# The first expert pair's tokens gathered as rows and then transposed, and the end of the routing in another order

## The chip, the cores and the metric

The kernel runs on one core of a Trainium2 chip. Its time is in device microseconds (us), the median of several runs. The engines are named as in the profile: PE (TensorE), DVE (VectorE), ACT (ScalarE), POOL (GpSimd) and SP (SyncE, which issues most DMAs).

## The reference

One decoder layer over 512 tokens of 1024 features, in float32: two mixers (dilated attention and a spatial gating unit), an output projection, a layer norm (LN1), a mixture of experts and a second layer norm. Here only the seam between LN1 and the experts matters:

```python
h = layer_norm(ALPHA * h + mix, ln1_g, ln1_b)          # 512 x 1024
g_logits = t @ w_group + b_group                        # 4 groups, the best one is taken
e_logits = einsum('td,gde->tge', t, w_expert) + b_expert
top_vals, top_idx = top_k(e_sel, 2)                     # 2 of the 8 experts of that group
gu  = einsum('td,edf->tef', t, w_gate_up[g])            # 1024 -> 2 x 256
act = silu(gu[..., :256]) * gu[..., 256:] * gate
y  += einsum('tef,efd->td', act, w_down[g])             # 256 -> 1024
h = layer_norm(ALPHA * h + y, ln2_g, ln2_b)
```

There are 32 experts. Each token goes to two of them, and all experts' weights are read: 96 MB.

## The kernel before

**Stages.** The input projection, attention and the gating unit come first. Then the output projection works in four tiles of 128 tokens (`i` = 0 to 3, `L` = 3); the first half of the features of all tiles comes first, and the loop at line 954 makes the second half tile by tile and carries LN1 and the routing of the tile before along with it. Behind the loop stands the end of the routing (lines 995 to 1046), then the expert loop over 16 pairs of experts.

**Slots and lists.** Each expert has 64 places, so a pair of experts is one tile of 128 rows. `route_pick` takes a tile's two experts per token (`A`, `Ab`), `route_rank` counts with small matmuls how many tokens went to each expert before (`rks`), `route_slots` makes each token's place, and `pair_sel(p, a, b)` (line 873) writes the 0/1 mask of pair `p` for tiles `a` to `b`, 8 x 128 columns for all four. `pair_list` (line 878) multiplies the mask with `vals` in 8 small matmuls and gives the token numbers (columns 0 to 3) or the gates (3 to 7) of the 128 rows. `pair_tok` turns them into indices, and `gather(p)` fetches the rows from `h_dram` into `xgs[p % 2]` with an indirect DMA that POOL issues.

**The first pair** has no gather. `slots_of(i)` makes `S0[i]` (line 916), the mask of pair 0 for tile `i` (128 tokens x 128 places), and `spread` multiplies with it on PE: `x_sb` of the tile, every eighth column from column `k`, is the stationary operand and `S0[i]` the moving one, so the product is the transposed input of feature block `k`, ready for the gate products. Eight blocks by four tiles make 32 such products. Tiles 0 to 2 are summed in `parts[0]` and `parts[1]`, which ACT copies to `x0f`; tile 3 goes to `parts[2]` and `parts[3]`, and DVE adds it (line 1041).

**The end of tile 3** is a chain over several engines: residual and statistics (DVE, lines 700 and 701), transposes (PE, line 708) with an ACT copy (709), `ln1_stats`, scaling by ACT (734) and POOL (737, 738) for columns 256 to 1023, `logit_mm` (715), `logit_out` (753, 754), `route_pick`, `ln1_rest` for columns 0 to 255 (744, 746), `h_out` (the tile's rows to `h_dram`, by SP), `route_rank`, `route_slots` (843 to 845), `slots_of`.

**The weights** lie in a ring of 21 slots of 1 MB, six fills to a pair. `wfill(n)` issues the fills up to number `n` on SP's queue, each waiting until its slot is free. Slot 19 is the room of `ln1_g` and `ln1_b`; fills 20 and 21 reuse the slots of pair 0's first four gate products (line 905, `k` = 0 to 3); fill 22 needs the room of the routing's tiles, which is closed behind `k` = 7, and the fills after it the slots that pair 0's later products free.

**Order.** From the middle of the output projection the instructions of PE, DVE, ACT, POOL and SP each run in the order in which the program writes them; nothing is rescheduled.

Of the kernel before, what the change touches and what calls it, by code (L numbers as in the profile page):

```python
# [10 lines left out]
F32 = mybir.dt.float32  # L11
# [14 lines left out]
NT = 4  # L26
KD = 8
# [31 lines left out]
def layer(tc, I, out):  # L59
# [41 lines left out]
    def ps_t():  # L101
        return ps_tp.tile([128, 4, 128], F32, name="tp", bufs=2)
# [600 lines left out]
    def r_transpose(i, n):  # L703
        rTs[i, n] = op.tile([128, 4, 128], F32, name="rT", bufs=2)
        tp = ps_t()
        for j in range(4):
            k = n * 4 + j
            pe.transpose(out=tp[:, j], in_=x_sb[:, i, k * 128:(k + 1) * 128], identity=ident)
        act.copy(rTs[i, n], tp)
# [6 lines left out]

    mv1s = {}

    def ln1_stats(i):
        mv1 = op.tile([128, 6], F32, name="mv1", bufs=4)  # L720
        mv1s[i] = mv1
        dve.bn_aggr(mv1[:, 0:2], st1[:, i])
        act.activation(mv1[:, 2:3], mv1[:, 1:2], AF.Sqrt, bias=eps)
        dve.tensor_scalar(mv1[:, 4:5], mv1[:, 0:1], -1.0, None, op0=ALU.mult)
        dve.reciprocal(mv1[:, 3:4], mv1[:, 2:3])
        dve.tensor_tensor(mv1[:, 5:6], mv1[:, 4:5], mv1[:, 3:4], op=ALU.mult)

    def ln1_apply(i, cut):

# [18 lines left out]
    def h_out(i):  # L748
        sp.dma_start(out=h_dram[i * 128:(i + 1) * 128, :], in_=x_sb[:, i])
# [92 lines left out]
    def route_slots(i):  # L842
        dve.tensor_tensor(t2, A[:, i], bc(rks[0][:, i, None, :], [128, 2, NE]), op=ALU.mult)
        dve.tensor_reduce(slot[:, i], t2, axis=AX.X, op=ALU.add)
        dve.tensor_tensor(slotp[:, :, i], bc(slot[:, i, None, :], [128, NPAIR, 2]), bc(iota_p[:, :, None], [128, NPAIR, 2]),
                          op=ALU.add)
# [64 lines left out]
    def slots_of(i):  # L911
        pair_sel(0, i, i + 1)
        if not S0:
            t = op.tile([128, NT, 128], F32, name="S0")
            S0.extend(t[:, j] for j in range(NT))
        dve.tensor_tensor(S0[i], sels[0][:, 2 * i], sels[0][:, 2 * i + 1], op=ALU.add)

    def spread(acc, k, tiles, start=True, stop=True):
        for i in tiles:
            pe.matmul(acc[:, k % 4 * 128:k % 4 * 128 + 128], x_sb[:, i].rearrange("s (q k) -> s k q", k=KD)[:, k], S0[i],  # L920
                      start=(start and i == tiles[0]), stop=(stop and i == tiles[-1]))

    for kk, k in enumerate(KORD):
        if kk == 4:
# [29 lines left out]
    for i in range(NT):  # L954
        for kk in range(KD):
            if i == L - 1 and kk == 4:

                for z in range(2):
                    op_second(L, z)
                wfill(15)  # L960
            op_second(i, kk)
            if i == 1 and kk == 0:
                router_sums()
            if i > 0 and kk == (1 if i < L else 2):
                r_transpose(i - 1, 1)
            if i > 0 and kk == (3 if i < L else 4):
                logit_mm(i - 1, 1)
                logit_out(i - 1)
                route_pick(i - 1, i)
                ln1_apply(i - 1, 512 if i < L else 0)  # L970
                if i < L:
                    ln1_rest(i - 1, 512)
            if i == L and kk == 3:
                wfill(17)
            if i == L and kk == 6:
                wfill(18)
            if kk == 5:
                r_transpose(i, 0)
            if kk == 7:
                logit_mm(i, 0)  # L980
                if i > 0:
                    route_rank(i - 1, i)
        resid(i, 1, acc1[i])
        if i < L:
            ln1_stats(i)
        if i > 0:
            route_slots(i - 1)
            slots_of(i - 1)
            if i < L:
                h_out(i - 1)  # L990
                for p in (1, 2):
                    pair_sel(p, i - 1, i)
        if i < L:
            wfill((13, 14, 16)[i])
    xg12 = opA.tile([128, 2, D], F32, name="xg12", tag="wo3")
    xgs = [xg12[:, p] for p in range(2)]
    h_out(L - 1)
    wfill(19)
    r_transpose(L, 1)
    ln1_stats(L)  # L1000
    xT0 = [op.tile([128, 4, 128], F32, name="rT", bufs=2) for _ in range(2)]
    x0f = [t.rearrange("p k s -> p (k s)") for t in xT0]
    parts = [ps_acc() for _ in range(4)]

    def part(ks):
        for k in ks:
            spread(parts[k // 4], k, range(L))

    ln1_apply(L, 256)
    act.preload_act_table(AF.Exp)  # L1010
    for k in (0, 4):
        spread(parts[k // 4], k, [0, 1], stop=False)
    logit_mm(L, 1)
    logit_out(L)
    route_pick(L, NT)
    for k in (0, 4):
        spread(parts[k // 4], k, [2], start=False)
    part([1, 2, 3])
    act.copy(x0f[0], parts[0])
    ln1_rest(L, 256)  # L1020
    h_out(L)
    route_rank(L, NT)
    route_slots(L)
    slots_of(L)
    part([5, 6, 7])
    act.copy(x0f[1], parts[1])
    for k in range(4):
        spread(parts[2], k, [L])
    for p in (1, 2):
        pair_sel(p, L - 1, NT)  # L1030
    ip0 = ps_t().rearrange("p a b -> p (a b)")
    ips = [ip0[:, 8 * p:8 * p + 7] for p in range(3)]
    for p in (1, 2, 0):
        pair_list(p, ips[p], 0, 3)
    for k in range(4, KD):
        spread(parts[3], k, [L])
    dve.tensor_tensor(emask, rks[0], bc(iota_c[:, None, :], [128, NT, NE]), op=ALU.is_ge)


    for kk in range(2):  # L1040
        dve.tensor_tensor(x0f[kk], x0f[kk], parts[2 + kk], op=ALU.add)
        pair_tok(kk + 1, ips[kk + 1], 1)
        gather(kk + 1)
    pair_tok(0, ips[0], 1)
    route_gates(0, NT)
    act.preload_act_table(AF.Silu)

    gp = ps_acc()
    for k in range(KD):
        gate_up(0, xT0, k, gp)  # L1050
        if k == 3:
            wfill(1 + NSLOT)
        if k == 0:
            pair_sel(3, 0, NT)
        if k == 5:
            cmax_i = route_spill()
        if k == 6:
            for p in range(3):
                pair_list(p, ips[p], 3, 7)
            for p in range(3):  # L1060
                dve.tensor_reduce(tgs[p][:, 1:2], ips[p][:, 3:6], axis=AX.X, op=ALU.add)
                pair_out(p, ips[p])
# [304 lines left out]
```

## Time and profile before

| | |
|---|---|
| median of 3 runs | 501.38 us (501.13 to 502.98) |
| the profiled execution | 501.38 us, its span 499.7 us |
| mean granted PE clock | 0.981 |
| PE busy | 468.3 us (94%) |
| DVE, ACT, POOL busy | 231.0, 162.4, 129.2 us |
| DMA | 141.18 MB, mean 283 GB/s |
| the chain that ended last | PE 65%, DMA 25%, DVE 6% |

Times in the rows count from the span's start. PE is the matmuls, PEld the loads of their stationary operand; a float32 matmul leaves two records of each, and the two halves of a gate product (two experts, 64 places each) run side by side. `PEclk` is the granted clock as a share of 2.4 GHz. A line of the timeline may merge several instructions (x8), and its time then reaches from the first start to the last end.

### The profile page before, as it was taken

How to read it: one execution, taken by the hardware profiler on the slowest of the kernel's cores; microseconds unless marked ns; L12 is line 12 of the kernel's file. 1: busy time of each engine (PE TensorE's matmuls, PEld its weight loads, DVE VectorE, ACT ScalarE, POOL GpSimd, SP SyncE). 2: the span in 40 equal slices, each digit the busy share in tenths (PEclk: the TensorE clock that was granted, in tenths of full speed). 3: DMA queues.
4: the chain of work that ended last, by engine and by line, in shares of the span. 5: the costliest groups of instructions: out<-in, count | busy, mean ns of one | idle time of the engine just before them, and what ended most of it. 6: DMA issues, size and time to landing. Idle time of an engine off the chain costs nothing.

```text
span 499.7 us, 6653 instructions
## 1 busy us (share of the span) xinstructions
PE 468.3 (94%) x2322; PEld 280.8 (56%) x2322; DVE 231.0 (46%) x598; ACT 162.4 (33%) x366; POOL 129.2 (26%) x196
## 2 busy tenths in 40 slices
PE   7999999999899999987999999999998898799994
PEld 5788887888767678867843333333333233243351
DVE  3586637723477638798452222222234331010146
ACT  4543536241478632322112222222221121032243
POOL 4024345000296910344111211111110110000380
PEclk9999999999999999998899999999999999898998
DMA  8844231750298549585589999999999999998464
GB/s 262 288 125 114 63 121 42 221 200 0 65 402 254 190 161 364 201 282 245 169 324 378 428 419 419 419 420 422 421 420 419 420 426 419 419 423 373 151 241 171
DMA packets 40805, 141.18 MB, mean 283 GB/s; under 512 B 10508, under 2 KB 14656, under 8 KB 28993
## 3 DMA queue, kind: packets, MB, share of 16 engines
q1 hardware_dynamic: 35808, 130.71, 68.3%
q0 software_dynamic: 4960, 10.01, 5.5%
q8 instruction: 20, 0.33, 0.3%
q14 instruction: 17, 0.13, 0.1%
HBM read 131.78 MB, written 16.25 MB: 296 GB/s over the span
## 4 chain that ended last, share of the span: by engine, by line
PE 65%; DMA 25%; DVE 6%; ACT 1%; SPq 1%; issue 1%; POOL 1%; ACTq 0%; DVEq 0%
DMA wc<-in_w_gate_up 14%; PE acc L905 13%; DMA wc<-in_w_down 9%; PE acc L320 7%; PE acc L321 7%; PE acc L322 7%; PE acc L1112 6%; PE acc L920 3%; DMA x_sb<-in_x 2%; PE tp L1082 2%; PE acc L605 2%; PE tp L620 2%; PE acc L580 1%; PE acc L582 1%; PE acc L581 1%; PE sc L414 1%
## 5 line engine op out<-in xcount | busy, mean ns | idle before, releaser
L905 PE MATMUL acc<-wc,xTm 128*64 128x512 f32 x464 | 120.6, 608 | 8.3 <-DMA wc<-in_w_gate_up 8.0
L905 PEld LDWEIGHTS acc<-wc,xTm 128*64 128x64 f32 x464 | 33.3, 138 | 72.2 <-issue 52.8
L320 PE MATMUL acc<-w_hi,xTh 128*128 128x512 f32 x160 | 65.1, 407 | 0.8 <-ACT vs_sb L375 0.7
L321 PE MATMUL acc<-w_lo,xTh 128*128 128x512 f32 x160 | 62.9, 393 | 0.4 <-DVE w_lo L312 0.4
L322 PE MATMUL acc<-w_hi,xTl 128*128 128x512 f32 x160 | 62.8, 392 | 0.0
L1112 PE MATMUL acc<-wc,aT 128*64 128x512 f32 x240 | 60.0, 610 | 2.9 <-ACT aT L1097 2.9
L1122 POOL DMA_INDIRECT y_dram<-y,to x15 | 15.8, 1053 | 140.4 <-DVE xTm L1083 74.2
L1120 DVE TENSOR_SCALAR rs<-rs 128x1 f32<-128x1 f32 x15 | 3.2, 214 | 91.9 <-ACT y L1114 91.9
L312 DVE TENSOR_TENSOR w_lo<-w_raw,w_hi 128x512 fp32r<-128x512 f32 x40 | 28.2, 706 | 34.5 <-ACT w_hi L311 34.3
L311 ACT ACTIVATE w_hi<-w_raw 128x512 fp32r<-128x512 f32 x40 | 25.3, 634 | 53.2 <-PE acc L322 47.8
L1112 PEld LDWEIGHTS acc<-wc,aT 128*64 128x64 f32 x240 | 18.6, 140 | 34.3 <-issue 30.3
L1114 ACT ACTIVATE y<-acc 128x512 f32<-128x512 f32 x30 | 17.9, 597 | 60.7 <-PE acc L1112 44.3
L422 POOL TENSOR_TENSOR P<-P,st 128x128 f32<-128x128 f32 (+3 forms) x32 | 23.2, 749 | 50.8 <-DVE st L421 49.3
L320 PEld LDWEIGHTS acc<-w_hi,xTh 128*128 128x128 f32 x160 | 30.2, 189 | 7.8 <-ACT vs_sb L375 1.1
L321 PEld LDWEIGHTS acc<-w_lo,xTh 128*128 128x128 f32 x160 | 30.2, 189 | 6.9 <-DVE w_lo L312 1.4
L1088 DVE SCALAR_TENSOR_TENSOR sa<-sa,tg,acc 128x256 f32<-128x256 f32 x16 | 7.7, 479 | 56.9 <-ACT sa L1087 53.0
L322 PEld LDWEIGHTS acc<-w_hi,xTl 128*128 128x128 f32 x160 | 30.0, 188 | 6.7 <-DVE xTl L163 0.3
L897 POOL DMA_INDIRECT xg<-h_dram,ti x15 | 15.8, 1053 | 56.2 <-DVE ti L894 19.5
L1087 ACT ACTIVATE sa<-acc 128x256 f32<-128x256 f32 x16 | 6.2, 385 | 69.1 <-PE acc L905 69.1
L1082 PEld LDWEIGHTS tp<-ident,xg 128*128 128x128 f32 x120 | 15.1, 194 | 18.7 <-issue 8.9
L873 DVE TENSOR_TENSOR sel<-iota_v,slotp 128x1024 bf16<-128x1024 f32 (+2 forms) x23 | 22.5, 990 | 0.1
L420 ACT ACTIVATE P<-P,st 128x128 f32<-128x128 f32 (+3 forms) x32 | 17.9, 563 | 8.3 <-DVE st L418 8.2
(334 smaller groups left out, 781.0 us busy)
## 6 DMA issues: line engine op xcount, KB each, us to landing
wc<-in_w_gate_up SPq DMA_DIRECT2D x62, 1024.0 KB, 19.2
wc<-in_w_down SPq DMA_DIRECT2D x30, 1024.0 KB, 20.8
w_raw<-in_w_in SPq DMA_DIRECT2D x18, 512.0 KB, 3.7
y_dram<-zeros SPq DMA_DIRECT2D x8, 512.0 KB, 8.0
wo_raw<-in_w_out SPq DMA_DIRECT2D x16, 256.0 KB, 3.5
wc<-y_dram SPq DMA_DIRECT2D x8, 512.0 KB, 9.3
x_sb<-in_x SPq DMA_DIRECT2D x8, 256.0 KB, 9.4
h_dram<-x_sb SPq DMA_DIRECT2D x4, 512.0 KB, 3.0
```

Source lines behind the costliest of these rows:

```text
L311: act.activation(wh, raw, AF.Copy)
L312: dve.tensor_tensor(wl, raw, wh.bitcast(F32), op=ALU.subtract)
L320: pe.matmul(acc[i], xh, wh, start=(k == 0), stop=False)
L321: pe.matmul(acc[i], xh, wl, start=False, stop=False)
L322: pe.matmul(acc[i], xl, wh, start=False, stop=(k == KD - 1))
L420: act.activation(P[:, 0:n], P[:, 0:n], AF.Exp, bias=st4[:, 0:1], scale=-1.0, accum_out=st4[:, 1:2])
L422: pool_e.tensor_tensor(P[:, 0:n], P[:, 0:n], bc(st4[:, 2:3], [128, n]), op=ALU.mult)
L873: dve.tensor_tensor(sels[p][:, 2 * a:2 * b], bc(iota_v.rearrange("p a b -> p (a b)")[:, None, :], [128, n, 128]), bc(slotp[:, p, a:b].rear ...
L905: pe.matmul(gp[zs], xT[k // 4][:, k % 4, zs], w[k % 4 // 2][:, k % 2 * 512:k % 2 * 512 + 512], start=(k == 0), stop=(k == KD - 1))
L1082: pe.transpose(out=tp[:, j], in_=xv[:, kk * 4 + j], identity=ident)
L1112: pe.matmul(dp[n][zs], aT[:, c, zs], w[c][:, ns], start=(c == 0), stop=(c == 1))
L1114: act.activation(y0[:, ns], dp[n], AF.Copy, accum_out=rs[:, n:n + 1])
```

## The change

Tile 0 of pair 0 is still spread. Tiles 1 to 3 are gathered as rows instead: `rows(i, ...)` multiplies the stationary `S0[i]` with 512 columns of `x_sb`, two products to a tile, summed over the three tiles in `parts[2]` and `parts[3]`. ACT and DVE copy the sum into `xgs[0]`, PE transposes it in eight blocks, and DVE adds them to the spread part of tile 0. The masks of pairs 1 and 2 are made for all tiles at once behind the routing, no longer tile by tile in the loop. The ranking and the slots of tile 2 move out of the loop's last turn to behind it, between spreads of tile 0, and the slots stand between the two parts of `ln1_stats(L)`. The list and the gather of pair 1 come ahead of the transposes. The lists of pairs 2 and 0, gather 2, `route_gates` and the table load follow gate product `k` = 1, and pair 3's mask follows `k` = 3. `wfill(20)` stands behind the last `h_out`; fills 20 and 21 stay behind `k` = 3. `ip0` is taken from the pool `ps_s` instead of `ps_t`.

```diff
-    def ln1_stats(i):
-        mv1 = op.tile([128, 6], F32, name="mv1", bufs=4)
-        mv1s[i] = mv1
-        dve.bn_aggr(mv1[:, 0:2], st1[:, i])
-        act.activation(mv1[:, 2:3], mv1[:, 1:2], AF.Sqrt, bias=eps)
-        dve.tensor_scalar(mv1[:, 4:5], mv1[:, 0:1], -1.0, None, op0=ALU.mult)
...
+    def ln1_stats(i, part=None):
+        if part in (None, 0):
+            mv1s[i] = op.tile([128, 6], F32, name="mv1", bufs=4)
+        mv1 = mv1s[i]
+        if part in (None, 0):
+            dve.bn_aggr(mv1[:, 0:2], st1[:, i])
+            act.activation(mv1[:, 2:3], mv1[:, 1:2], AF.Sqrt, bias=eps)
+        if part in (None, 1):
+            dve.tensor_scalar(mv1[:, 4:5], mv1[:, 0:1], -1.0, None, op0=ALU.mult)
...
-    def spread(acc, k, tiles, start=True, stop=True):
-        for i in tiles:
-            pe.matmul(acc[:, k % 4 * 128:k % 4 * 128 + 128], x_sb[:, i].rearrange("s (q k) -> s k q", k=KD)[:, k], S0[i],
-                      start=(start and i == tiles[0]), stop=(stop and i == tiles[-1]))
+    def spread(i, k):
+
+        pe.matmul(parts[k // 4][:, k % 4 * 128:k % 4 * 128 + 128], x_sb[:, i].rearrange("s (q k) -> s k q", k=KD)[:, k], S0[i],
+                  start=True, stop=True)
+
+    def rows(i, first, last):
+
+        for n in range(2):
+            pe.matmul(parts[2 + n], S0[i], x_sb[:, i, n * 512:n * 512 + 512], start=first, stop=last)
...
-                if i > 0:
+                if 0 < i < L:
                     route_rank(i - 1, i)
         resid(i, 1, acc1[i])
         if i < L:
             ln1_stats(i)
-        if i > 0:
-            route_slots(i - 1)
-            slots_of(i - 1)
-            if i < L:
+            if i > 0:
+                route_slots(i - 1)
+                slots_of(i - 1)
                 h_out(i - 1)
-                for p in (1, 2):
-                    pair_sel(p, i - 1, i)
-        if i < L:
             wfill((13, 14, 16)[i])
...
+    parts = [ps_acc() for _ in range(4)]
+
+
+    for k in range(3):
+        spread(0, k)
+    route_rank(L - 1, L)
+    spread(0, 3)
     r_transpose(L, 1)
-    ln1_stats(L)
...
+    ln1_stats(L, 0)
+    route_slots(L - 1)
+    slots_of(L - 1)
+    ln1_stats(L, 1)
     ln1_apply(L, 256)
     act.preload_act_table(AF.Exp)
-    for k in (0, 4):
-        spread(parts[k // 4], k, [0, 1], stop=False)
+    for k in (4, 5):
+        spread(0, k)
     logit_mm(L, 1)
     logit_out(L)
     route_pick(L, NT)
-    for k in (0, 4):
-        spread(parts[k // 4], k, [2], start=False)
-    part([1, 2, 3])
-    act.copy(x0f[0], parts[0])
     ln1_rest(L, 256)
     h_out(L)
+    wfill(20)
+    for k in (6, 7):
+        spread(0, k)
...
+    for kk in range(2):
+        act.copy(x0f[kk], parts[kk])
+    rows(1, True, False)
+    rows(2, False, False)
     route_rank(L, NT)
     route_slots(L)
     slots_of(L)
-    part([5, 6, 7])
-    act.copy(x0f[1], parts[1])
-    for k in range(4):
-        spread(parts[2], k, [L])
-    for p in (1, 2):
-        pair_sel(p, L - 1, NT)
-    ip0 = ps_t().rearrange("p a b -> p (a b)")
+    pair_sel(1, 0, NT)
+    rows(L, False, True)
+    for n in range(2):
+        (dve.tensor_copy if n else act.copy)(xgs[0][:, n * 512:n * 512 + 512], parts[2 + n])
+    ip0 = ps_s()
     ips = [ip0[:, 8 * p:8 * p + 7] for p in range(3)]
-    for p in (1, 2, 0):
-        pair_list(p, ips[p], 0, 3)
-    for k in range(4, KD):
-        spread(parts[3], k, [L])
-    dve.tensor_tensor(emask, rks[0], bc(iota_c[:, None, :], [128, NT, NE]), op=ALU.is_ge)
-
-
+    pair_list(1, ips[1], 0, 3)
+    pair_tok(1, ips[1], 1)
+    gather(1)
     for kk in range(2):
-        dve.tensor_tensor(x0f[kk], x0f[kk], parts[2 + kk], op=ALU.add)
-        pair_tok(kk + 1, ips[kk + 1], 1)
-        gather(kk + 1)
-    pair_tok(0, ips[0], 1)
-    route_gates(0, NT)
-    act.preload_act_table(AF.Silu)
+        tp = ps_t()
+        for j in range(4):
+            pe.transpose(out=tp[:, j], in_=xgs[0].rearrange("s (q k) -> s k q", k=KD)[:, kk * 4 + j], identity=ident)
+        dve.tensor_tensor(x0f[kk], x0f[kk], tp.rearrange("p k s -> p (k s)"), op=ALU.add)
+    pair_sel(2, 0, NT)
+
 
     gp = ps_acc()
     for k in range(KD):
         gate_up(0, xT0, k, gp)
+        if k == 1:
+            pair_list(2, ips[2], 0, 3)
+            pair_tok(2, ips[2], 1)
+            gather(2)
+            pair_list(0, ips[0], 0, 3)
+            pair_tok(0, ips[0], 1)
+            dve.tensor_tensor(emask, rks[0], bc(iota_c[:, None, :], [128, NT, NE]), op=ALU.is_ge)
+            route_gates(0, NT)
+            act.preload_act_table(AF.Silu)
         if k == 3:
             wfill(1 + NSLOT)
-        if k == 0:
             pair_sel(3, 0, NT)
```

## Rows read from the trace of the kernel before

**Rows 1.** the page's slices of 12.5 us: DMA busy share in tenths.

```profile
DMA  8844231750298549585589999999999999998464
```

**Rows 2.** windows: us, PE, PEld, DVE, ACT, POOL busy (x), PEclk, DMA share, GB/s.

```profile
251.65:321.00 69.35, 69.15 (x390) 26.91 (x388) 21.05 (x57) 13.98 (x36) 12.22 (x13) 1.00 1.00 402
321.00:433.00 112.00, 101.79 (x502) 37.79 (x500) 34.20 (x70) 21.06 (x55) 16.41 (x16) 1.00 1.02 421
```

**Rows 3.** the chain that ended last: start us, us, what.

```profile
409.46 23.29 DMA wc<-in_w_gate_up
432.80 5.34 PE acc L905 x14
```

**Rows 4.** timeline of SyncE's queue: start us, us, what [idle before <-releaser].

```profile
237.96 0.42 SPq L532 DMA_DIRECT2D wc19g<-in_w_gate_up  x1
...
251.65 1.06 SPq L534 DMA_DIRECT2D wc<-in_w_gate_up  x2
256.32 0.81 SPq L534 DMA_DIRECT2D wc<-in_w_down  x2
```

**Rows 5.** timeline, all engines, the tile loop of the output projection.

```profile
212.03 1.55 POOL L738 TENSOR_TENSOR x_sb<-x_sb,ln_b 128x512 f32<-128x512 f32 x1
...
214.07 0.26 DVE L754 SCALAR_TENSOR_TENSOR lg<-lg,mv,lb 128x40 f32<-128x40 f32 x1
...
218.36 0.66 PE L708 MATMUL tp<-ident,x_sb 128*128 128x128 f32 x4 [1.00 <-DVE x_sb L700]
...
222.29 1.85 DVE L873 TENSOR_TENSOR sel<-iota_v,slotp 128x256 bf16<-128x256 f32 x2
...
223.82 1.44 POOL L737 TENSOR_TENSOR x_sb<-x_sb,ln_g 128x512 f32<-128x512 f32 x1
...
224.34 0.98 DVE L754 SCALAR_TENSOR_TENSOR lg<-lg,mv,lb 128x40 f32<-128x40 f32 x1
...
227.79 0.68 DVE L700 SCALAR_TENSOR_TENSOR x_sb<-x_sb,acc 128x512 f32<-128x512 f32 x1
```

**Rows 6.** timeline, all engines, the end of the routing.

```profile
227.92 0.18 PE L822 MATMUL sc<-Ab,tri 128*128 128x32 bf16 x1 [2.38 <-DVE Ab L815]
...
228.52 1.11 PE L708 MATMUL tp<-ident,x_sb 128*128 128x128 f32 x4 [0.40 <-DVE x_sb L700]
...
232.64 0.26 DVE L753 SCALAR_TENSOR_TENSOR lg<-csum,mv,sc 128x40 f32<-128x40 f32 x1 [1.22 <-PE sc L715]
...
238.07 0.22 DVE L843 TENSOR_TENSOR t<-A,sc 128x64 f32<-128x64 bf16 x1 [0.55 <-PE sc L823]
...
239.27 0.29 DVE L916 TENSOR_TENSOR S<-sel 128x128 f32<-128x128 bf16 x1
```

**Rows 7.** the chain that ended last: spread products, and 512-column products of the tail.

```profile
232.60 5.32 PE acc L920 x22
...
472.65 0.86 PE sc L1158 x2
```

**Rows 8.** windows: GpSimd (POOL) on tile 3, columns as in rows 2.

```profile
232.00:244.00 12.00, 12.00 (x59) 11.99 (x59) 7.29 (x22) 3.23 (x5) 4.01 (x4) 1.00 0.45 144
```

**Rows 9.** timeline and DMA issues, from the spreads to the first gate product.

```profile
242.54 0.59 ACT L1026 COPY rT<-acc 128x512 f32<-128x512 f32 x1 [3.94 <-PE acc L920]
...
244.19 0.75 PE L878 MATMUL tp<-vals,sel 128*128 128x3 bf16 x24
...
246.99 6.35 PE L905 MATMUL acc<-wc,rT 128*64 128x512 f32 x24
...
xg<-h_dram,ti POOLq DMA_INDIRECT x2, 4.6
```

**Rows 10.** windows and chain: gate products at either clock.

```profile
246.00:249.00 3.00, 3.00 (x11) 1.53 (x12) 1.48 (x8) 0.36 (x2) 1.47 (x2) 0.50 0.48 127
...
247.06 6.28 PE acc L905 x24
...
445.75 6.87 PE acc L905 x32
```

More of the change, by code (lines that the diff above doesn't have):

```diff
@@ L717, in layer @@
     mv1s = {}
-    def ln1_stats(i):
-        mv1 = op.tile([128, 6], F32, name="mv1", bufs=4)
-        mv1s[i] = mv1
-        dve.bn_aggr(mv1[:, 0:2], st1[:, i])
-        act.activation(mv1[:, 2:3], mv1[:, 1:2], AF.Sqrt, bias=eps)
-        dve.tensor_scalar(mv1[:, 4:5], mv1[:, 0:1], -1.0, None, op0=ALU.mult)
-        dve.reciprocal(mv1[:, 3:4], mv1[:, 2:3])
-        dve.tensor_tensor(mv1[:, 5:6], mv1[:, 4:5], mv1[:, 3:4], op=ALU.mult)
+    def ln1_stats(i, part=None):
[7 more added lines that the diff above has]
+            dve.tensor_scalar(mv1[:, 4:5], mv1[:, 0:1], -1.0, None, op0=ALU.mult)
+            dve.reciprocal(mv1[:, 3:4], mv1[:, 2:3])
+            dve.tensor_tensor(mv1[:, 5:6], mv1[:, 4:5], mv1[:, 3:4], op=ALU.mult)
     def ln1_apply(i, cut):
@@ L998, in layer @@
     wfill(19)
-    r_transpose(L, 1)
-    ln1_stats(L)
[L1001 to L1007, printed above, removed]
+    parts = [ps_acc() for _ in range(4)]
[3 more added lines that the diff above has]
+    spread(0, 3)
+    r_transpose(L, 1)
+    ln1_stats(L, 0)
+    route_slots(L - 1)
+    slots_of(L - 1)
+    ln1_stats(L, 1)
     ln1_apply(L, 256)
     act.preload_act_table(AF.Exp)
-    for k in (0, 4):
-        spread(parts[k // 4], k, [0, 1], stop=False)
+    for k in (4, 5):
+        spread(0, k)
     logit_mm(L, 1)
@@ L1015, in layer @@
     route_pick(L, NT)
-    for k in (0, 4):
-        spread(parts[k // 4], k, [2], start=False)
-    part([1, 2, 3])
-    act.copy(x0f[0], parts[0])
     ln1_rest(L, 256)
     h_out(L)
+    wfill(20)
+    for k in (6, 7):
+        spread(0, k)
+    xT0 = [op.tile([128, 4, 128], F32, name="rT", bufs=2) for _ in range(2)]
+    x0f = [t.rearrange("p k s -> p (k s)") for t in xT0]
+    for kk in range(2):
+        act.copy(x0f[kk], parts[kk])
+    rows(1, True, False)
+    rows(2, False, False)
     route_rank(L, NT)
```

## The prediction

> **What bounds the kernel now.** I read the page's slices first (12.5 us each): DMA stands at 9 tenths in the 22nd to 36th and at 5 in the two that end at 250 us [rows 1]. The plateau is the stream of expert weights. The windows confirm it: from 251.65 to 433 us the DMA share is 1.00 to 1.02 at 402 to 421 GB/s, while TensorE is busy 101.8 of 112 us in the second stretch [rows 2]. In the chain that ended last, the step that ends at 432.80 us is a weight transfer of this stream, and from there on it is TensorE that works off what landed [rows 3]. So the end lies a fixed distance behind the start of an unbroken stream. SyncE's queue says when that starts: 19 fills of 1 MB are issued early, the 20th goes out in two halves from 237.96 us, and the next two wait until 251.65, when the fourth gate product of pair 0 has freed their slots; the fills behind the eighth product follow at 256.32 [rows 4]. The change is worth what it moves those two times by.
>
> **The change part by part.** I follow the time of each event, before and after.
>
> Part 1, the masks of pairs 1 and 2. Two groups of two L873 leave the tile loop on VectorE; the group that stands in the rows took 1.85 us, the other as much [rows 5]. GpSimd normalises a tile at that time, and VectorE's rows stretch beside it: L754 takes 0.98 us there and ends just behind GpSimd's L737 (223.82 + 1.44), where it takes 0.26 alone [rows 5]. So part of what is freed is waited away. First group: L754 of tile 1 can move up only to GpSimd's end at 212.03 + 1.55 = 213.58 and finish by some 213.6, not at 214.33: 0.7 us. TensorE's idle 1.00 us ahead of tile 2's transposes lets all that follows, GpSimd's four instructions too, come 0.7 us earlier [rows 5]. Second group: L754, L807 and L814 then each wait for one of the four, the last until about 225.9, and the residual L700 of tile 3 starts at 226.05, not at 227.79 [rows 5]: 1.7 us, not 2 x 1.85. The Trainium skill, "SBUF — State Buffer", on the port pair that VectorE and GpSimd share, calls it an exclusive lock, and says that a VectorE instruction with two SBUF inputs is held for the whole of a GpSimd instruction that reads SBUF. By that rule the trace's 0.98 against 0.26 is no accident; without it part 1 would be worth 3.7 us and the forecast stand at about 493.5.
>
> Part 2, the logits of tile 3. TensorE now idles 2.38 us for `route_rank` of tile 2 [rows 6]. In its place come three spread products of tile 0, whose operands are ready; one is two records, 0.48 us (22 records in 5.32 us [rows 7]). The transposes of tile 3 move from 228.52 to about 226.9 [rows 6], two spreads stand behind them instead of four, and the logits are done by 229.5. VectorE does `bn_aggr`, then the five instructions for tile 2's slots (1.5 us before too, now in another order), then the three of the statistics, to 229.65. `logit_out` starts there and not at 232.64 [rows 6]: 3.0 us.
>
> Part 3, S0 of tile 3. From 232.64 until L843 at 238.07 lie the picking and `ln1_rest`, and at their end 0.55 us of waiting for TensorE [rows 6]. GpSimd's four instructions for tile 3 take 4.01 us [rows 8]: they start at 230.4, behind the scale, and end at 234.5. The picking ends at 232.3; L744 and L746 read two SBUF operands, so I let them finish behind GpSimd, at 235.0. Meanwhile TensorE has two spreads, rows(1), rows(2) and `route_rank`: a product of 512 columns takes 0.86 us (L1158 in the tail [rows 7]), so 229.5 + 1.0 + 4 x 0.86 + 0.4 = 234.3, just under that cover; if the clock is low there, 3.4 us of it come through. L843 to L916 take 1.5: S0 is ready at 236.4, before at 239.56 [rows 6]. Gain 3.2. Should `ln1_rest` pass GpSimd it is 235.8; should only part 1's 1.7 us carry through, 237.8.
>
> Part 4, from S0 to the first gate product. Before, 239.56 to 246.99: 7.4 us. TensorE was still 2.9 us behind with spreads of tiles 0 to 2 (ACT took the last at 242.54), then came four spreads, 24 list products and four spreads [rows 9]. After: rows(3) 1.7 us, with pair 1's whole mask beside it on VectorE; the second half's copy 0.7 (as L700's 0.68, 512 columns from PSUM [rows 5]); four transposes 0.6 (0.66 in [rows 5]); `pair_tok`, 0.35, which stands ahead of the addition but beside the transposes; the addition 0.7; handovers 0.3: 4.0 us. The second half's transposes lie under the first addition. Gate product 0 starts at 240.4: 6.6 us earlier. Of 24 spreads that leave (11.6 us) and six products of rows that come (5.2 us), what counts is the backlog and the piece behind S0; what stood ahead of S0 only filled waits.
>
> Part 5, to the fourth gate product. Before, 246.99 to 251.65: 4.66 us. Six products took 6.28 where eight take 6.87 at full clock, 0.86 each, so 1.1 us was lost to the granted clock of 0.50 (1.2 GHz) between 246 and 249 us [rows 10]. After: 4 x 0.86 = 3.4, plus the lists of pairs 2 and 0 between the second and third product, 16 of the small products (24 took 0.75 us [rows 9]), 0.5, plus 0.2 to SyncE: 4.1. Pair 2's mask is made behind the additions, S0 + 4.7 + 1.2, about when product 1 ends (S0 + 5.7): at most 0.3 us. I add 1.0 for a stretch at 1.2 GHz like today's: TensorE will have waited some 2 us for S0 and done small work, and today's fall came right behind 24 list products. 240.4 + 5.3 = 245.7: the refill goes out 5.9 us earlier.
>
> Part 6, the rest. `wfill(20)` changes nothing: on SyncE the 20th fill already goes ahead of the refills [rows 4]. `route_gates` (13 instructions of about 0.2 us, as L753's 0.26) and `pair_sel(3)` come behind gathers' lists on VectorE; the gates are ready at S0 + 9.9, 246.3, and wanted by the lists behind product 6, at some 248. That work of TensorE's is their cover; without it the last product, and the fills of 256.32, would slip by as much. Gather 1 goes out near 239.6; its transposes come behind product 7, near 250; two gathers took 4.6 us to land [rows 9]. The last `h_out`, which it must follow, is issued at 235.1. Gather 2 stands on GpSimd's queue at 243.4 and is wanted 15 us later; it now meets the first refill, at most by its own 0.5 MB, 1.2 us at 420 GB/s. Pair 3's mask on VectorE, 1.2 us, still precedes its list by over 2 us. Product 7 ends near 250, over 6 us earlier, so the second batch of fills moves as the first.
>
> **Sum.** The profiled execution took 501.38 us with a span of 499.7; it is also the median (501.13 to 502.98). 501.38 - 5.9 = 495.5. Unknown: S0 (+0.6, -1.4 us of gain), the clock at full throughout or low for 3 us more (+1.0, -1.5), gather 2 in the stream (0, -1.2): gains from some 2.6 (not all the losses at once) to 7.5.
>
> **Rivals.**
> (a) VectorE's freed time is waited away at GpSimd in tile 3 as well. For: L754 ends with GpSimd's instruction. Against: GpSimd starts when the scale is there, which comes earlier too. S0 then comes at 237.8, gain 4.5, 496.9.
> (b) The clock is at 1.2 GHz from rows(3) through product 3. For: the wait ahead of rows(3), and today's fall at much the same work. Against: it lasted only until 249. Price: two products of 512 columns 1.7, four gate products 3.4, less the 1.0 in the sum: gain 1.8, 499.6.
> (c) Slower: the low clock outlasts the gate products. By product 7, rows(3) and eight products have lost 8.6 us against a gain of 7.0 at full clock; there it turns. Through four products of pair 1, 3.4 more: 501.4 + 1.6 + 3.4 = 506.4. Against: gate products had the clock back at 1.00 within 3 us [rows 10].
> (d) The stream does not set the end, and nothing changes: 501.4. Against: [rows 2, 3].
>
> **How the numbers follow.** 0.62 for the forecast (alone 493.8 to 496.9), 0.20 for (a), 0.08 for (b), 0.06 for (c), 0.04 for (d). A measurement of this kernel can tell about 0.5%, 2.5 us, from no change. Faster by more: the forecast and (a), 0.82; the same: (b) and (d), 0.12; slower: (c), 0.06. The range, 493.5 to 498.8, takes in the forecast and (a) with the unknown costs and leaves out (b) to (d), 0.18.
>
> **What would show it.** Right, if SyncE issues two refills near 245.7 us and the next fills near 250, gate product 0 starts near 240.4, S0 of tile 3 is done near 236.4, `logit_out` of tile 3 starts near 229.7, its L700 near 226, and the plateau ends 6 us earlier. Wrong, if gate product 0 comes after 242.5, if the granted clock is 0.5 for over 4 us around it, if pair 1's transposes wait for their gather, or if the refills come earlier and the plateau ends where it does now.

## The result and the profile after

The changed kernel takes 496.56 us (median of 4, 495.56 to 497.09) against 501.26 for the kernel before (median of 4): a ratio of 0.9886, interval 0.9856 to 0.9916. A later measurement of both kernels (e8 below) gave 496.60 against 501.36, ratio 0.9919, interval 0.9889 to 0.9948. Both intervals lie clear of 1; the gain is about 1%. The profiled execution took 496.95 us with a span of 495.2.

The page's slices, beside [rows 1]: the plateau of the DMA engines starts a slice earlier. The granted clock does not drop in the seam any more; the second line is that of the kernel before, where slices 19 and 20 stand at 8.

```profile
PEclk9999999999999999999999999999999999997998
```

```profile
PEclk9999999999999999998899999999999999898998
```

```profile
DMA  8743231570099568587699999999999999997454
```

SyncE's queue, beside [rows 4]. The two refills go out at 245.85 us (5.80 earlier), the second batch at 250.53 (5.79 earlier), and the last fills of the stream, which stood at 446.14 before, at 440.83 (5.31 earlier).

```profile
245.85 0.80 SPq L534 DMA_DIRECT2D wc<-in_w_gate_up  x2
250.53 0.80 SPq L534 DMA_DIRECT2D wc<-in_w_down  x2
...
440.83 2.82 SPq L534 DMA_DIRECT2D wc<-in_w_down  x2
```

The tile loop, beside [rows 5]. L754 is L757 now, L753 is L756. Both L757 of the loop take 1.08 us and end with GpSimd's L741 (212.63 + 1.30 and 221.95 + 1.29): the masks are gone, and VectorE now waits for GpSimd at both turns (the first L754 took 0.26 us before), only earlier.

```profile
211.44 1.26 DVE L919 TENSOR_TENSOR S<-sel 128x128 f32<-128x128 bf16 x1
...
212.63 1.30 POOL L741 TENSOR_TENSOR x_sb<-x_sb,ln_b 128x512 f32<-128x512 f32 x1
212.90 1.08 DVE L757 SCALAR_TENSOR_TENSOR lg<-lg,mv,lb 128x40 f32<-128x40 f32 x1
...
221.95 1.29 POOL L741 TENSOR_TENSOR x_sb<-x_sb,ln_b 128x512 f32<-128x512 f32 x1
...
222.22 1.08 DVE L757 SCALAR_TENSOR_TENSOR lg<-lg,mv,lb 128x40 f32<-128x40 f32 x1
...
226.08 0.68 DVE L700 SCALAR_TENSOR_TENSOR x_sb<-x_sb,acc 128x512 f32<-128x512 f32 x1
```

The end of the routing, beside [rows 6]. TensorE's 2.38 us of idling for `route_rank` are down to 0.37. In tile 3's picking L818, a 128x32 bfloat16 addition that takes 0.17 to 0.18 us elsewhere in the same profile, takes 1.25 us and ends with GpSimd's last instruction; S0 of tile 3 is ready at 236.34 + 0.29 = 236.63.

```profile
226.22 0.18 PE L825 MATMUL sc<-Ab,tri 128*128 128x32 bf16 x1 [0.37 <-DVE Ab L818]
...
229.33 0.25 DVE L756 SCALAR_TENSOR_TENSOR lg<-csum,mv,sc 128x40 f32<-128x40 f32 x1
...
233.03 1.26 POOL L741 TENSOR_TENSOR x_sb<-x_sb,ln_b 128x512 f32<-128x512 f32 x1
233.07 1.25 DVE L818 TENSOR_TENSOR Ab<-A 128x32 bf16<-128x32 bf16 x1
...
236.34 0.29 DVE L919 TENSOR_TENSOR S<-sel 128x128 f32<-128x128 bf16 x1
```

From S0 to the gate products, beside [rows 9]: rows(3), the copy, the transposes, the addition, the first products.

```profile
236.78 1.95 PE L929 MATMUL acc<-x_sb,S 128*128 128x512 f32 x4 [2.20 <-DVE S L919]
...
238.77 0.69 DVE L1039 COPY xg<-acc 128x512 f32<-128x512 f32 x1 [1.00 <-PE acc L929]
...
239.61 1.13 PE L1048 MATMUL tp<-ident,xg 128*128 128x128 f32 x8 [0.69 <-DVE tg L892]
...
240.40 1.29 DVE L1049 TENSOR_TENSOR rT<-rT,tp 128x512 f32<-128x512 f32 x2 [0.68 <-PE tp L1048]
...
241.15 1.94 PE L908 MATMUL acc<-wc,rT 128*64 128x512 f32 x8 [0.41 <-issue]
```

And the chain at the end, beside [rows 3]: a transfer of the stream still releases it, now at 443.30 us.

```profile
424.71 18.55 DMA wc<-in_w_gate_up
443.30 3.65 PE acc L908 x14
446.95 1.09 PE tp L1095 x8
...
451.19 6.60 PE acc L1125 x16
...
459.70 7.02 PE acc L908 x32
```

The same chain of the kernel before:

```profile
452.62 1.09 PE tp L1082 x8
...
456.86 5.35 PE acc L1112 x16
...
464.13 7.02 PE acc L905 x32
```

Pair 14's gate products end 5.67 us earlier (452.62 to 446.95), pair 15's begin only 4.43 earlier, and the span is 4.5 shorter. The 1.24 us between lie in pair 14's down products: 6.60 us against 5.35. The granted clock was 0.50 for 6.5 us there, and 0.51 over 3.3 us in the kernel before; first after, then before, columns as in [rows 2]:

```profile
450.50:457.00 6.50, 5.81 (x14) 1.72 (x16) 0.00 (x0) 1.14 (x4) 0.00 (x0) 0.50 0.67 284
```

```profile
457.40:460.70 3.30, 3.30 (x10) 0.96 (x8) 0.00 (x0) 0.38 (x1) 0.00 (x0) 0.51 0.79 328
```

### The profile page after: what moved, and what is told of

It is laid out like the page before. It is cut to its first block, busy times and chain, and to the rows that moved or that the text cites. A ratio compares the mean times of both kernels' runs of the same rounds, so it can differ in the third digit from the quotient of the medians.

```text
span 495.2 us, 6597 instructions
## 1 busy us (share of the span) xinstructions
PE 462.3 (93%) x2294; PEld 272.4 (55%) x2294; DVE 231.1 (47%) x595; ACT 162.3 (33%) x367; POOL 128.3 (26%) x196
## 4 chain that ended last, share of the span: by engine, by line
PE 52%; DMA 38%; DVE 7%; ACT 1%; issue 1%; SPq 1%; DVEq 0%; ACTq 0%
DMA wc<-in_w_gate_up 25%; PE acc L320 7%; PE acc L322 7%; PE acc L321 7%; PE acc L908 7%; DMA wc<-in_w_down 4%; DMA wc19b<-in_w_down 4%; PE acc L1125 3%; DMA x_sb<-in_x 2%; PE acc L605 2%; PE tp L620 2%; PE acc L580 1%; PE acc L582 1%; PE acc L581 1%; DMA w_raw<-in_w_in 1%; DMA wo_raw<-in_w_out 1%
## 5 line engine op out<-in xcount | busy, mean ns | idle before, releaser
L1125 PE MATMUL acc<-wc,aT 128*64 128x512 f32 x240 | 61.3, 622 | 2.9 <-ACT aT L1110 2.9
L900 POOL DMA_INDIRECT xg<-h_dram,ti x15 | 15.8, 1050 | 51.6 <-DVE ti L897 17.5
L580 PE MATMUL acc<-wo,mT 128*128 128x512 f32 x48 | 20.3, 423 | 0.0
```

The costliest lines, as they stand in the source:

```text
L580: pe.matmul(acc, mh, wh, start=first, stop=False)
L900: pool_e.indirect_dma_start(out=xgs[p % 2], out_offset=None, in_=h_dram[:, :], in_offset=bass.IndirectOffsetOnAxis(ap=tis[p][:, 0:1], axis=0),
L1125: pe.matmul(dp[n][zs], aT[:, c, zs], w[c][:, ns], start=(c == 0), stop=(c == 1))
```

## The experiments

All runs are compared behind one mark, since what lies ahead of it moved by 3.5 us from execution to execution: the start of tile 0's S0 on VectorE (L916 before, L919 after; 210.2 to 213.7 us). All are edits of the changed kernel. The columns give when the event starts, for S0 when it is ready; "second batch" is the fills behind the eighth product.

| behind tile 0's S0, us | tile 3's L700 | S0 of tile 3 | gate product 0 | refills | second batch | last fills | end of span |
|---|---|---|---|---|---|---|---|
| before | 16.95 | 28.72 | 36.15 | 40.81 | 45.48 | 235.30 | 288.86 |
| changed | 14.64 | 25.19 | 29.71 | 34.41 | 39.09 | 229.39 | 283.76 |
| changed, again (e8) | 14.64 | 25.14 | 29.65 | 34.36 | 39.04 | 229.03 | 282.19 |
| e1 masks in the loop | 16.96 | 28.62 | 33.13 | 37.83 | 42.51 | 232.26 | 285.38 |
| e2 spreads | 14.64 | 25.21 | 32.83 | 37.54 | 42.22 | 231.86 | 285.22 |
| e3 refills late | 14.65 | 26.34 | 30.86 | 37.28 | 40.24 | 231.21 | 285.60 |
| e4 cut at 512 | 14.65 | 24.71 | 29.16 | 33.87 | 38.55 | 228.38 | 281.56 |
| e5 lists late | 14.65 | 25.20 | 31.12 | 35.71 | 41.41 | 231.39 | 284.30 |
| e6 tail filled | 14.65 | 25.21 | 30.55 | 36.74 | 41.41 | 231.38 | 282.15 |
| e7 all three | 14.65 | 26.32 | 30.77 | 34.45 | 40.43 | 230.02 | 280.94 |
| e9 filler | 14.66 | 25.14 | 29.65 | 34.36 | 39.04 | 229.06 | 280.80 |
| e10 cut and tail | 14.65 | 24.72 | 29.16 | 33.87 | 38.55 | 228.49 | 278.99 |
| e11 filler, cut and tail | 14.65 | 24.72 | 29.17 | 33.88 | 38.56 | 228.45 | 279.26 |

The granted clock has a hand in these times. Between 222 and 250 us it stayed at 1.00 in the profiles of the changed kernel, e8, e4, e9, e10 and e11, and fell to 0.50 in the others: twice for about 3.4 us in the kernel before (from 228.5 and from 245.6), once for 3.4 us in e2 (from 229.6, with S0 where it was) and once for about 6.8 us in e1, e3, e5, e6 and e7.

**e1, the masks back in the loop.**

```diff
                 h_out(i - 1)
+                for p in (1, 2):
+                    pair_sel(p, i - 1, i)
...
-    pair_sel(1, 0, NT)
+    pair_sel(1, L - 1, NT)
...
-    pair_sel(2, 0, NT)
+    pair_sel(2, L - 1, NT)
```

> The changed kernel, with the masks of pairs 1 and 2 for tiles 0 and 1 made in the tile loop again (two L876 of 256 columns behind each of two tiles); only tiles 2 and 3 are left for behind the routing. Theory (part 1 of the prediction): the four masks sit on VectorE's chain beside GpSimd, so tile 3's L700 starts near 227.8 us instead of 226.08, S0 of tile 3 ends 1.5 to 1.7 us later than 236.63, the first two refills go out near 247.4 instead of 245.85, and the kernel takes 1.5 us more, some 498.3. Rival (the freed time is waited away behind GpSimd anyway): L700 within 0.5 us of 226.08 and no change of the time.

Measured: 498.69 us, ratio 0.994 (0.9915 to 0.9966). L700 falls back to where it stood before the change, 16.96 us behind the mark. The 1.85 us of [rows 5] are there again, one such group in each of two turns, and together they cost the path 2.32 us.

```profile
222.77 1.85 DVE L876 TENSOR_TENSOR sel<-iota_v,slotp 128x256 bf16<-128x256 f32 x2
...
228.28 0.68 DVE L700 SCALAR_TENSOR_TENSOR x_sb<-x_sb,acc 128x512 f32<-128x512 f32 x1
```

S0 of tile 3 came 3.43 us later, more than expected: in this profile the clock fell to 0.50 between 229 and 235.5 us, as in e3, where that fall alone cost S0 1.15. So about 2.3 us are the masks', as L700, which lies ahead of the fall, says by itself; the theory stands, and so does part 1, with a larger size. The median is 2.1 us above the changed kernel's (1.5 were expected). That is not the clock's doing: at a mean clock of 0.988 three runs of e1 took 498.31 to 498.61 us, and three of the changed kernel 496.17 to 496.42.

**e2, spreads instead of rows, in the new order.**

```diff
...
-    rows(1, True, False)
-    rows(2, False, False)
+    act.copy(x0f[0], parts[0])
     route_rank(L, NT)
+    for k in (5, 6, 7):
+        for i in range(L):
+            spread(i, k)
...
-    rows(L, False, True)
+    for k in range(KD):
+        spread(L, k)
```

> The changed kernel in its new order, but tiles 1 to 3 of pair 0 spread in 24 products of 128 columns as before, with no rows, no copies and no transposes of pair 0; route_rank of tile 3 stands after 10 of them. Theory: the rows themselves are worth little beside the new order. 14 spreads of 0.48 us stand from about 234 us on, so TensorE is at tile 3's spreads near 239 and at the first gate product near 243.0 instead of 241.15; refills near 247.7; the kernel takes 1.5 to 2 us more, some 498.4. Rival (part 4 of the prediction read as a sum of the rows alone: 3.4 us for the piece behind S0): first gate product at 244.5 or later, 500 us. If the granted clock falls to 0.5 at the gate products, as it did in the kernel before behind its lists, another 1.1 us.

Measured: 499.11 us, ratio 0.9951 (0.9929 to 0.9973). S0 is where it was, 25.21, and gate product 0 comes 3.1 us later: the theory's 1.85 was too little, the rival's 3.35 (244.5 us for 241.15) is nearly reached, and the time lies between the two. TensorE is through the spreads only at 243.6, and as the list, its indices and the addition follow one another here, it then waits 1.04 us for VectorE.

```profile
235.21 8.38 PE L923 MATMUL acc<-S,x_sb 128*128 128x128 f32 x34
243.43 0.34 PE L881 MATMUL sc<-vals,sel 128*128 128x3 bf16 x8
244.81 1.94 PE L908 MATMUL acc<-wc,rT 128*64 128x512 f32 x8 [1.04 <-DVE rT L1048]
```

So the rows, with the order of the list that goes with them, are worth 3.1 us of the path up to gate product 0, about 2 of it TensorE's backlog and 1 the wait behind the list. Masks (2.3) and rows (3.1) leave 1.0 of the 6.4 us by which gate product 0 moved behind the mark. It falls to the rest of the new order and to the clock; no run takes that order back by itself.

**e3, the refills late.**

```diff
-    for k in range(KD):
-        gate_up(0, xT0, k, gp)
+    for k, kp in enumerate((0, 1, 2, 4, 5, 3, 6, 7)):
+        gate_up(0, xT0, kp, gp)
...
         if k == 3:
-            wfill(1 + NSLOT)
             pair_sel(3, 0, NT)
         if k == 5:
+            wfill(1 + NSLOT)
```

> The changed kernel, with pair 0's eight gate products in the order 0, 1, 2, 4, 5, 3, 6, 7: the slots of fills 20 and 21 come free two products later, and nothing else is added. Theory (the stream's start sets the end): the two refills go out near 247.7 us instead of 245.85, and the kernel takes 1.5 to 2 us more, some 498.4. Rival (the fills behind the eighth product, 250.53 us, set the stream, and the first two have room): the time within 0.5 us of the changed kernel's 496.6.

Measured: 499.12 us, ratio 0.9925 (0.9893 to 0.9957), in the profile 285.60 behind the mark. From gate product 0 to the refills it is 6.42 us instead of 4.70, the 1.72 of two products. But the clock fell too, between 229 and 235.5 us, ahead of anything that the edit touches (the instructions up to there are the same):

```profile
229.00:235.50 6.50, 6.50 (x25) 5.37 (x25) 4.83 (x19) 4.44 (x7) 2.95 (x4) 0.50 0.75 311
```

That moved everything from S0 on by 1.15 us. Behind the mark the second batch is 1.15 later, the refills 2.87, the last fills 1.82. So 0.67 of the 1.72 came through to the last fills (0.98 if e8 is the base): neither theory, the stream hangs on both, and more on the second batch. In the time nothing of it can be told. The higher median is the clock's: with a mean clock of 0.985 to 0.991 three runs of e3 took 495.60 to 497.61 us and eight of the changed kernel 495.56 to 497.09; at 0.979 three and four runs, 499.12 to 500.96 and 498.95 to 500.94. The 1.5 to 2 us of the theory are not there.

**e4, LN1 of tile 3 cut at column 512.**

```diff
-    ln1_apply(L, 256)
+    ln1_apply(L, 512)
...
-    ln1_rest(L, 256)
+    ln1_rest(L, 512)
```

> The changed kernel, with tile 3's LN1 cut at column 512 instead of 256: GpSimd has two instructions of 512 columns instead of four, VectorE's L747 and L749 have 512 columns instead of 256 (0.5 us more work). Theory (VectorE waits for GpSimd's instructions in tile 3's picking, L817 1.34 and L818 1.25 us instead of 0.2): GpSimd is through near 233.0 us instead of 234.3, the picking ends near 233.2, S0 of tile 3 ends at 236.1, 0.5 us earlier, and the kernel takes 0.3 to 0.5 us less. Rival (only VectorE's own work counts): S0 ends 0.5 us later, 237.1, and the kernel takes 0.5 us more.

Measured: 495.99 us, ratio 0.9877 (0.9843 to 0.991); S0 0.48 us earlier behind the mark, refills 0.54, with 0.5 us more work on VectorE. L818 is back at 0.18 us: it starts when GpSimd is through, which is 1.27 us earlier behind the mark. That is the theory; only VectorE's own work, the rival, would have made S0 later.

```profile
232.69 1.33 POOL L741 TENSOR_TENSOR x_sb<-x_sb,ln_b 128x512 f32<-128x512 f32 x1
```

```profile
234.13 0.18 DVE L818 TENSOR_TENSOR Ab<-A 128x32 bf16<-128x32 bf16 x1
```

So what VectorE pays for is its wait behind GpSimd, and a little more work of its own that shortens this wait is a gain. The Trainium skill, "SBUF — State Buffer", section "Who interferes with whom", says that a VectorE instruction with two SBUF inputs contends with a GpSimd instruction that reads SBUF. The trace agrees: both inputs of L818 lie in SBUF, and it takes 1.25 us beside L741 and 0.18 behind it. The time itself is too near the changed kernel's to be told apart; the profile is not.

**e5, the lists late; e6, the tail filled; e7, both with the cut; e8, the changed kernel again.** They ran on one chip.

```diff
         if k == 1:
+            dve.tensor_tensor(emask, rks[0], bc(iota_c[:, None, :], [128, NT, NE]), op=ALU.is_ge)
+            route_gates(0, NT)
+            act.preload_act_table(AF.Silu)
+        if k == 3:
+            wfill(1 + NSLOT)
             pair_list(2, ips[2], 0, 3)
             pair_tok(2, ips[2], 1)
...
             pair_list(0, ips[0], 0, 3)
             pair_tok(0, ips[0], 1)
-            dve.tensor_tensor(emask, rks[0], bc(iota_c[:, None, :], [128, NT, NE]), op=ALU.is_ge)
-            route_gates(0, NT)
-            act.preload_act_table(AF.Silu)
-        if k == 3:
-            wfill(1 + NSLOT)
             pair_sel(3, 0, NT)
```

This is e5: the lists leave the place behind product 1 and stand behind the refill. And e6:

```diff
-        if p == LAST:
-            for n in range(2):
-                fin_x(2, n)
...
-            down(p, act_transposed(sa))
+            aT = act_transposed(sa)
+            if p == LAST - 1:
+                for n in range(2):
+                    fin_x(2, n)
+            down(p, aT)
```

> The changed kernel, with the lists of pairs 2 and 0, their indices and gather 2 behind gate product 3 instead of product 1, and the gates ahead of them on VectorE. Theory: from gate product 0 to the refill 3.8 us instead of 4.70, the second batch of fills 0.3 us earlier at most; as the first two fills were seen to pass on only a part of a delay (0.7 of 1.7 us in the run with the refill late), the kernel takes 0.3 to 0.6 us less. Rival (the second batch alone counts): within 0.3 us.

> The changed kernel, with the two products of tile 2's last sum (L1171, 512 columns each) put into pair 14's wait for ACT's copy instead of ahead of pair 15's gate products. Theory (the 1.3 us that are gained at the refill and missing at the end were lost to a longer stretch at 1.2 GHz around pair 14's down products, which took 6.60 us instead of 5.35): with TensorE at work in that wait, the products of pair 14 start up to 0.9 us later but pair 15's gate products at least 0.8 us earlier than 459.70 less the run's own shift; if the clock stays up, 1.5 us more. The kernel takes 0.8 to 2.3 us less. Rival (the weights of the last pairs set the end): pair 15's gate products wait for DMA and the time stays.

> The three edits together (LN1 of tile 3 cut at column 512, the lists late, the tail's products in the wait). Theory: they lie on different pieces of the path and add up: S0 0.5 us earlier, the refill 1.4 us earlier relative to tile 0's S0, the end 1.5 to 3 us earlier than the changed kernel on the same chip. Rival: the end stays within 0.5 us of the changed kernel, since the stream's own 420 GB/s and the clock of the tail take it back.

> The changed kernel itself on the chip of the three others, so that they stand beside it: 0.985 to 0.992 of the kernel before. Its seam holds the same instructions as the run with the refill late up to the gate products; in that run the clock was at 0.50 from 229 us on and S0 of tile 3 came 1.15 us later behind tile 0's S0 than in the changed kernel's profile. If that is chance, this run may show either, and S0 of tile 3 comes 25.2 us behind tile 0's L919 with the clock at 1.00 and 26.3 with it at 0.50.

Measured: e5 497.10 us, ratio 0.9903 (0.9868 to 0.9939); e6 494.36, 0.9851 (0.9813 to 0.9889); e7 493.92, 0.9858 (0.9819 to 0.9897); e8 496.60, 0.9919 (0.9889 to 0.9948).

e5 and e6 happen to make a pair. In both the clock fell from 237.5 to 244 us (in e5 on instructions that lie half a microsecond earlier, so that its gate product 0 comes 0.57 us later), and the second batch lies 41.41 us behind the mark in both. The refills lie at 35.71 and 36.74. The last fills: 231.39 and 231.38. First e5, then e6:

```profile
237.50:244.00 6.50, 5.82 (x23) 2.90 (x23) 3.21 (x7) 0.59 (x1) 1.16 (x1) 0.50 0.69 209
```

```profile
246.91 0.80 SPq L534 DMA_DIRECT2D wc<-in_w_gate_up  x2
252.61 0.80 SPq L534 DMA_DIRECT2D wc<-in_w_down  x2
...
442.59 2.82 SPq L534 DMA_DIRECT2D wc<-in_w_down  x2
```

```profile
237.50:244.00 6.50, 5.82 (x25) 2.66 (x23) 3.42 (x6) 0.12 (x1) 1.16 (x1) 0.50 0.65 216
```

```profile
247.29 0.80 SPq L534 DMA_DIRECT2D wc<-in_w_gate_up  x2
251.96 0.80 SPq L534 DMA_DIRECT2D wc<-in_w_down  x2
...
441.93 2.83 SPq L534 DMA_DIRECT2D wc<-in_w_down  x2
```

So refills that go out 1.03 us earlier are worth nothing when the second batch stays: e5's rival. The whole table says so: from the second batch to the last fills it is 189.6 to 190.3 us in every profile but e3's (191.0), while from the refills it is 193.9 to 195.7. The second batch sets the stream, as long as the refills are 4.7 us or more ahead of it; at 3.0 us (e3) they cost some.

In e6 pair 15's gate products start 14.9 us behind the last fills (456.80 against 441.93); in e8 it is 17.5, and in the changed kernel's profile 18.9 (459.70 against 440.83). Of this, 1.4 is the clock: e8 is the same kernel, with 0.50 for 3.3 us instead of 6.5 and 5.18 us for the down products instead of 6.60. The rest, 2.6, comes with the edit: 1.6 because pair 14's down products take 3.58 us, at full clock, and 1.0 because the two products stand in a wait. The clock goes with the edit in all profiles: these down products took 3.58 us in the four that have it (e6, e7, e10, e11), 5.06 to 6.60 in eight of the nine that lack it, and 3.65 in the ninth (e9). First e8, then e6:

```profile
450.80:454.10 3.30, 3.08 (x8) 1.00 (x10) 0.00 (x0) 0.16 (x1) 0.00 (x0) 0.50 0.80 338
```

```profile
451.01 5.18 PE acc L1125 x16
...
458.11 7.02 PE acc L908 x32
```

```profile
451.50 1.72 PE tp L1171 x4
453.22 3.58 PE acc L1125 x16
456.80 7.20 PE acc L908 x32
```

That not all of the stream's gain arrived is thus the clock of the tail. e6 takes 2.2 us less than e8, as expected (0.8 to 2.3). e7 meets its expectation for the time (2.7 us less than e8; 1.5 to 3), but came out no clearly better than e6, and its S0 was late: its profile had the clock at 0.50 in the seam from 226.3 to 233 us, and its lists late are worth nothing by e5. e8 lies where it was expected, with S0 at 25.14 and the clock at 1.00.

**e9, filler products; e10, the cut and the tail; e11, all three.**

```diff
+    def filler(*cols):
+        t = ps_t().rearrange("p a b -> p (a b)")
+        for n in cols:
+            pe.matmul(t[:, 0:n], ident, x_sb[:, 0, 0:n], start=True, stop=True)
...
+    filler(256)
     route_rank(L - 1, L)
...
+    filler(512, 512)
     rows(L, False, True)
...
     gather(1)
+    filler(256)
```

> The changed kernel with four extra products on TensorE whose results nobody reads, in the gaps in which it waits: one of 256 columns ahead of route_rank of tile 2, two of 512 ahead of rows(3), one of 256 ahead of the transposes of pair 0 (2.6 us in all at full clock). Theory: the two groups in which the runs of the changed kernel lie (495.5 to 496.6 us at a mean clock of 0.985 and more, 499.0 to 500.9 at 0.979 to 0.984) differ by a fall of the granted clock to 0.50 for 3.5 to 7 us in the seam, and it comes behind those gaps (from 229 us on behind the one at 226, from 237.5 on behind the one at 234.6 to 236.8). Filled, the clock stays at 1.00 from 222 to 250 us, S0 of tile 3 lies 25.2 to 25.6 us behind tile 0's L919, the second batch of fills 39 to 39.6 us behind it, and the slow group is gone or rare: median 0.986 to 0.990 of the kernel before. Rival (the falls have another cause, or the filler only costs): as many runs in the slow group, or the second batch 1 us and more later at full clock.

> The changed kernel with LN1 of tile 3 cut at column 512 and the tail's two products of tile 2 in pair 14's wait. Theory: the second batch of fills 38.6 us behind tile 0's L919 where the clock stays up in the seam (39.1 in the changed kernel), 40 to 41 where it falls; from the last fill to the end 50.9 us instead of 53.2 to 54.4; the kernel at 0.982 to 0.986 of the kernel before. Rival: the tail's gain is lost to a new wait for weights ahead of pair 15's gate products, 0.988 or more.

> The two edits of the run beside it and the filler products together. Theory: no fall of the clock in the seam, the second batch 38.6 to 39.2 us behind tile 0's L919, 50.9 us from the last fill to the end, and a narrow group of times: 0.980 to 0.985 of the kernel before, the lowest of all versions. Rival: the filler stands in the way of S0 or the transposes now that S0 comes 0.5 us earlier, and the time is that of the run without filler, or up to 1 us more.

Measured: e9 494.50 us, ratio 0.9875 (0.9844 to 0.9906); e10 493.13, 0.9843 (0.9819 to 0.9867); e11 492.31, 0.9832 (0.9804 to 0.986). The filler costs nothing: in e9 S0 lies 25.14 us behind the mark and the second batch 39.04, as in e8. Whether it holds the clock up stays open. In neither of the two profiles with it (e9, e11) did the clock fall between 222 and 250 us, but neither did it in four of the ten without it. Of the runs at a mean clock of 0.984 or less and 498 us or more there was 1 of 6 with the filler, and 5 of 11 in e8, none of 4 in the first measurement. That is too few to tell. e10 and e11 are clearly faster than the kernel before, and have lower medians than the changed one; the interval of e10, 0.9819 to 0.9867, lies nearly clear of the changed kernel's (0.9856 to 0.9916, then 0.9889 to 0.9948). Both meet their expectations: the second batch 38.55 and 38.56 us behind the mark, and 50.5 and 50.8 us from the last fills to the end. e10 and e11 themselves are not told apart by their intervals.

## Why the prediction was right, and where it was off

**Part 1** gave L700 of tile 3 at 226.05; it starts at 226.08. Behind the mark the gain is 2.31, not 1.74: this execution was 0.6 us late when it came to the mark. The mechanism held (both L757 end with GpSimd; e1), the term was 0.6 too small. I had the first group at 0.7, and it gave 0.95, since GpSimd's own L741 now took 1.30 us beside it instead of 1.55. The rest lies in the second group.

**Part 2**, `logit_out` at 229.65: 229.33. What I had not seen: in the kernel before the clock fell to 0.50 from 228.5 us on as well, ahead of the fall of [rows 10]. The transposes of tile 3 and the second half of the logits took 1.11 and 1.28 us there, and 0.65 and 1.02 after, so about 0.7 us of this part is the clock's.

```profile
228.50:232.00 3.50, 3.48 (x17) 3.48 (x17) 2.54 (x10) 1.42 (x4) 0.00 (x0) 0.51 0.98 392
```

**Part 3**, S0 at 236.4: 236.63. GpSimd was through at 234.29, as forecast (234.5). What it held up was the end of the picking, L817 (1.34 us) and L818 (1.25), which I had through at 232.3; L747, which I had waiting, only followed L818 at 234.25. Rival (a) fell: the waits are there, yet GpSimd came earlier as well.

**Part 4** was too short: 4.0 us forecast, 4.5 measured. From the start of rows(3) to that of the second half's copy it is 1.99 us (1.7 forecast), the copy is through at 239.46, 2.8 us behind S0, and from the start of the transposes to that of the addition it is 0.79 (0.6). The handovers are 0.36 (0.3). The 0.41 us ahead of gate product 0 lie under the addition, which ends at 241.09.

**Part 5** was too long: 5.3 forecast, 4.70 measured. The gate products took 0.86 each, the lists with their waits 0.9, where I had 0.5. The 1.0 us for a stretch at 1.2 GHz was not due in this profile; in e6, with the clock at 0.50 from 237.5 us, the same piece took 6.19. So the term exists, 1.5 us large, in some executions and not in others; in this one it covered for the 0.4 that the rest of the part lacked. And parts 4 and 5 made up for each other by luck: refills at 245.7 forecast, 245.85 measured.

**Part 6** held. That `wfill(20)` changes nothing was not run; in the program no other transfer stands on SyncE's queue between it and the refills. The gates were ready at 247.08 and wanted at 248.69; pair 1's transposes started without a wait for their gather.

**The sum** took 5.9 us at the refill as 5.9 at the end. Measured are 5.8 and 4.4 (profiled) or 4.7 (medians). The step that came out too large is "the end lies a fixed distance behind the start of the stream": pair 14's gate products still came 5.67 us earlier, and 1.24 were lost in the tail to a longer stretch at 0.50 (e8, the same kernel, gave them back). And of the two times that start the stream, it is the second batch that counts (e5, e6), not the refill that I summed on; both had moved by 5.8 and the last fills by 5.3, so the forecast did not suffer much. In absolute time the refill was also met by luck: this execution came 0.6 us late to the mark, and behind the mark refills and second batch moved by 6.4.

**What the clock has to do with the gain.** Part of these 6.4 us belongs to the clock: the kernel before had two falls in its seam, and the changed kernel's two profiles had none. Where one fall of about 6.8 us did strike the changed seam, the second batch lay 40.24 (e3) and 41.41 us (e6) behind the mark, 5.2 and 4.1 earlier than before. The times agree: over all runs whose clock is on record, those with a mean clock of 0.976 to 0.982 give a median of 501.37 us (29 runs) for the kernel before and 499.63 (4) for the changed one, those from 0.987 up 500.06 (3) and 496.17 (9). At a like clock the change is thus worth some 1.7 to 3.9 us, by few runs. The rest of the 4.7 goes with a higher mean clock of the changed kernel's runs (median 0.988 against 0.978); whether they owe that to the change is not shown.

**Rival (b)** is no single case but a matter of the execution: the fall at the gate products is real in e5 and e6, and there it cost the second batch 2.3 us. So a sign that I had named for being wrong, the clock at 0.5 for over 4 us around gate product 0, came true in them, and the second batch was still 4.1 us earlier than before. **(c)** was not seen: in no profile did a fall of the seam reach beyond product 2. **(d)** fell with the result, and with e1 and e2, where the stream came later and so did the end.

## What to carry to other kernels

Ahead of an unbroken stream of transfers, find the release that the stream really hangs on: hold one candidate, move the other, and read the last transfer's issue, not the end. An edit that frees an engine which is seen to wait for another is priced by where the other's instructions end. And when the same program gives two times, mark one event that no edit touches and count from there, and set beside each other only executions with a like granted clock; otherwise 1 to 2 us of the clock's luck are taken for the edit's.

## What the runs had not led me to expect

The granted clock is not a property of the program alone. The changed kernel's seam was at 1.00 throughout in two profiles. e3, with the same instructions up to the gate products, was at 0.50 from 229 to 235.5 us, though TensorE had waited no longer than 0.39 us at a time since 224 us:

```profile
228.49 0.18 PE L825 MATMUL sc<-Ab,tri 128*128 128x32 bf16 x1 [0.39 <-DVE Ab L818]
```

e5 and e6 were at 0.50 from 237.5 to 244, behind the same wait of 2.2 us that left it at 1.00 in the changed kernel:

```profile
234.60:236.80 2.20, 0.02 (x1) 0.05 (x1) 2.03 (x8) 0.00 (x0) 0.00 (x0) 1.00 0.33 130
```

The DMA engines are slow to fill behind a refill, but two fills of 1 MB are enough to do it. With the two refills out since 245.85 us the changed kernel moved 176 GB/s from 246 to 248 us and 352 in the next two, still ahead of the second batch at 250.53. The kernel before moved 418 from 254 to 256 us, with its refills out since 251.65 and its second batch still to come at 256.32. First after, then before:

```profile
246.00:248.00 2.00, 2.00 (x14) 0.65 (x12) 1.83 (x7) 0.30 (x1) 0.00 (x0) 1.00 0.83 176
248.00:250.00 2.00, 2.00 (x32) 0.87 (x28) 1.87 (x13) 0.00 (x0) 0.00 (x0) 1.00 0.95 352
```

```profile
254.00:256.00 2.00, 2.00 (x32) 0.87 (x28) 0.49 (x6) 0.00 (x0) 0.00 (x0) 1.00 1.02 418
```
